# Hybrid SSD and attention block on one core: the weight sums' place, the tiles of the third product and the last block of S2

## The chip, the core and the metric

The kernel runs on one core of a Trainium2 chip. Its engines work side by side, each through its own list of instructions in a fixed order: TensorE (PE, matmuls and transposes, results go to PSUM), VectorE (DVE), ScalarE (ACT), GpSimd (POOL) and SyncE (SP, which here issues the DMA transfers). The metric is the device time of one execution in microseconds (us), the median over several. The profile is of one further execution; its span runs from the first to the last instruction.

## What is computed

One layer: a norm, an input projection, a state-space scan (SSD) over half of the channels, differential attention over the other half, gates, and an output projection of the two halves together, with a residual and a final norm. What the change touches is the attention and the output projection:

```python
def block(args):
    s = jnp.einsum('bhmqd,bhmkd->bhmqk', qblk, kh)        # two maps m per head
    s = jnp.where(dist >= 0, s + bias, -jnp.inf)
    p = jax.nn.softmax(s, axis=-1)
    w = p[:, :, 0] - lam * p[:, :, 1]
    return jnp.einsum('bhqk,bhke->bhqe', w, vh)
...
y_attn = attn.reshape(bsz, seq, D_ATTN) * jax.nn.silu(z_attn)
mixed = jnp.concatenate([y_ssd, y_attn], axis=-1)         # 1024 x 2048
h = h + jnp.einsum('bse,ed->bsd', mixed, w_out)           # w_out: 2048 x 1024
return rms_norm(h, final_norm_gain)
```

Sequence and model width are 1024, there are 8 heads, everything is float32.

## The kernel before

**Precision.** A float32 product is made of three matmuls of a reduced type: each operand is split into a high part (ACT copies it into that type) and a low part (DVE subtracts the high part), and hi x hi, hi x lo and lo x hi are summed in PSUM. So every operand passes over ACT and DVE before PE can use it. Names ending in `hi`/`lo` or `h`/`l` are these parts.

**Stages.** After the norm come the scan's two groups, then eight attention heads in four pairs, each head in two halves of 512 query rows, and then the output projection. `attend` handles a half head: four row blocks of 128 queries. For each of them PE makes the scores of both maps (L557) into two PSUM tiles S, DVE evicts them with the mask and takes the maximum (L563), ACT takes the exponential (L581), DVE combines the two maps (L594), PE transposes the result through the one PSUM bank `tp` (L602), ACT copies it out as `wT` (L605), and PE multiplies it with v (L609). At the end of a half head DVE copies the result out as `oc` (L614), and ACT sums its squares (L617). `gate` later multiplies with the gate z (L641), transposes (L647), and ACT writes `tTa` (L649), which goes to DRAM as a block of `tt_d` (L651). `tt_d` holds the transposed left operand of the output projection: 16 blocks of 128 channels, in two halves of the sequence; the last block of attention, 15, comes from the last head. Between the steps of softmax PE works on projections of the next heads, which fill its time.

**The output projection** is one step of Strassen's method in the Winograd form, with seven products of 512 x 1024 by 1024 x 512. Its left operands are A11, A12, A22 and the sums S1 to S4 of quarters of the left matrix, its right operands B11, B21, B22 and the sums T1 to T4 of quarters of `w_out`. They run in the order a11·b11, s3·t3, a12·b21, s2·t2, s1·t1, s4·b22, a22·t4 (`product`, matmuls at L757 to L759). A product has four row blocks `i` of 128, each of 8 x 3 matmuls of 512 columns, into the two PSUM banks `mm`. `find_t(k)` makes the sums T for one block of 128 rows: four loads into K tiles, four subtractions or additions on DVE (L673 to L679), each written to `t_d`. S3 is found from two loaded pieces when it is needed (L724) and written to `s3_d`; S2 is found from A22 and S3 (L735), S1 and S4 from S2 (L740, L745). `prep_b` and `prep_a` load and split operands (hi on ACT L689 and L710, lo on DVE L690 and L711). The first two products fill PE's time during the last head. Results are added to the rows `xr` of the residual on DVE (L821, L858, L860); `end_row` sums the squares and multiplies with the gain `fg` (L834), `finish` multiplies with the row's factor (ACT L841, DVE L843) and writes the output.

**What sets the order.** A scheduler in the recording layer puts the instructions of each engine in a list, by its own estimate of times, by the program's order as priority, and by when a tile's buffer comes free; on the chip each engine goes through its list strictly. Tiles come from pools of a fixed number of buffers: K (4 of 512 columns x 128), A (4), B (3), G (13), H (5), raw (2), u (4). All DMA transfers stand in SP's list, and one that has to wait holds up those behind it.

Of the kernel before, what the change touches and what calls it, by code (L numbers as in the profile page):

```python
# [38 lines left out]
def kernel(  # L39
# [595 lines left out]
    def gate(h, half, normed, z):  # L635
# [15 lines left out]
        dma(td[k], tT)  # L651
# [16 lines left out]
    def find_t(k):  # L668

        b11, b12, b21, b22 = (tK([P, HALF], name=f"b{i}{j}{k}") for i in range(1, 3) for j in range(1, 3))  # L670
        for raw, i, j in ((b22, 1, 1), (b12, 0, 1), (b11, 0, 0), (b21, 1, 0)):
# [1 line left out]
        V.tensor_tensor(b12, b22, b12, ALU.subtract)  # L673
# [6 lines left out]
        dma(t_d[1][k], b22)  # L680

    def prep_b(name, src, makers):

        hi, lo = (big_tile("u", 4, [P, NB, HALF], F32R, f"{name}_{n}") for n in ("hi", "lo"))
        for k in range(0, NB, 2):
            raw = makers[k // 2]([P, 2, HALF], name=f"r{name}{k}")
            dma(raw, src[k : k + 2].rearrange("a p c -> p a c"))
            cut = slice(k, k + 2)
            A.activation(hi[:, cut, :], raw, AF.Copy)  # L689
            V.tensor_tensor(lo[:, cut, :], raw, hi[:, cut, :].bitcast(F32), ALU.subtract)  # L690
        return hi, lo

    def load_a(raw, th, kh, q, k0, n):

        k = k0
        while k < k0 + n:
# [3 lines left out]
            dma(raw[:, k - k0 : e - k0, :], src.rearrange("k p s -> p k s"))  # L700
            k = e

    def prep_a(name, q, step, piece):
# [3 lines left out]
        for k0 in range(0, NB, step):  # L707
            raw = piece(q, k0, step)
            cut = slice(k0, k0 + step)
            A.activation(hi[:, cut, :], raw, AF.Copy)  # L710
# [62 lines left out]
    for p in range(HEADS // 2):  # L773
# [49 lines left out]
    def end_row(t, n, c0=0, c1=HALF):  # L823
# [10 lines left out]
        V.tensor_tensor(xt, xt, fg[:, n * HALF + c0 : n * HALF + c1], ALU.mult)  # L834

    def finish(t):
        r = sm.tile([P, 1], F32, tag="rs1", name=f"r_f{t}")
        G.tensor_tensor(r, ss[t][:, 0:1], half_pow[:, :1], ALU.pow)
# [90 lines left out]
```

## Time and profile before

| | us |
|---|---|
| median of three runs | 1047.63 |
| the three runs | 1046.67, 1047.63, 1049.41 |
| the profiled execution | 1046.4 |
| its span | 1044.3 |
| TensorE busy in it (last matmul ends at 1038.0) | 1006.9 |
| VectorE busy | 660.3 |
| ScalarE busy | 532.0 |
| mean granted TensorE clock (1 is full) | 0.993 |

The page of the profile shows the busy share of each engine in 40 slices of the span (26 us each), in tenths, 9 standing for 90% or more; under them the granted clock of TensorE, and the DMA engines:

```profile
PE   6999999999999989999999999999999999888997
DVE  6556578755566567476373772646816867579973
ACT  8253467834456434456353563535634755553352
PEclk9999999999999999999999999999999999999999
DMA  7111124211224787322103221023202447796432
```

The scan runs up to about 350 us, the heads up to 919, the last five products behind them. The heads are best read by who waited for whom, the ends by a timeline.

### The profile page before, as it was taken

To read this page: it belongs to the slowest core of one execution; us is meant where nothing else is said; L and a number is where in the kernel's file an instruction comes from. 1 tells how busy PE (TensorE), PEld (TensorE's weight loads), DVE (VectorE), ACT (ScalarE), POOL (GpSimd) and SP (SyncE) were. 2 spreads that over 40 slices of the span, in tenths; PEclk is the share of its full clock that TensorE was granted. 3 is DMA by queue.
4 is the path that set the end of the run, shared out by engine and by line. 5 is a ranking of instruction groups with operands and counts; after the bars stand their busy time and mean duration, and the time that the engine had idled before them with its cause. 6 is when DMAs were issued, how large, how long until landed. Compare 5 with 4: busy or idle time off the path is not lost.

```text
span 1044.3 us, 16231 instructions
## 1 busy us (share of the span) xinstructions
PE 1006.9 (96%) x6214; PEld 891.7 (85%) x6214; DVE 660.3 (63%) x1357; ACT 532.0 (51%) x1147; POOL 93.3 (9%) x133
## 2 busy tenths in 40 slices
PE   6999999999999989999999999999999999888997
PEld 5988888879997988889998889988899898766886
DVE  6556578755566567476373772646816867579973
ACT  8253467834456434456353563535634755553352
POOL 6000023200222100000000000000000000000011
PEclk9999999999999999999999999999999999999999
DMA  7111124211224787322103221023202447796432
GB/s 292 41 63 41 61 72 131 81 61 61 99 83 134 248 285 242 82 74 68 52 12 81 61 81 49 14 62 81 82 11 71 142 159 226 249 323 212 155 127 101
DMA packets 64948, 119.34 MB, mean 114 GB/s; under 512 B 5403, under 2 KB 30440, under 8 KB 64872
## 3 DMA queue, kind: packets, MB, share of 16 engines
q1 hardware_dynamic: 64872, 118.31, 34.9%
q8 instruction: 49, 0.80, 0.3%
q14 instruction: 27, 0.22, 0.1%
HBM read 86.77 MB, written 23.13 MB: 105 GB/s over the span
## 4 chain that ended last, share of the span: by engine, by line
PE 48%; DMA 8%; DVE 8%; issue 3%; ACT 2%; SPq 0%; POOL 0%; POOLq 0%; DVEq 0%; ACTq 0%
PE o L609 5%; PE mm L210 4%; PE mm L208 4%; PE mm L209 4%; PE mm L217 4%; PE mm L218 4%; PE mm L219 4%; PE S L557 4%; DMA ra<-tt_d 3%; PE mm L757 3%; PE mm L758 3%; PE mm L759 3%; DMA b<-in_w_out_dram 3%; PE tp L602 2%; DMA t_d<-b 1%
## 5 line engine op out<-in xcount | busy, mean ns | idle before, releaser
L581 ACT ACTIVATE s<-s,small 128x256 f32<-128x256 f32 (+7 forms) x128 | 98.7, 772 | 96.0 <-DVE small L573 95.5
L563 DVE CUSTOM_DVE_ANT_0 s<-S,dist 128x256 f32<-128x256 f32 (+7 forms) x128 | 94.2, 753 | 33.8 <-PE S L557 31.2
L208 PE MATMUL mm<-uh,hi_qk 128*128 128x512 f32 x256 | 101.5, 397 | 0.0
L210 PE MATMUL mm<-uh,lo_qk 128*128 128x512 f32 x256 | 101.0, 394 | 0.0
L209 PE MATMUL mm<-ul,hi_qk 128*128 128x512 f32 x256 | 100.7, 393 | 0.0
L557 PE MATMUL S<-k,q 128*128 128x512 f32 (+2 forms) x384 | 90.6, 358 | 4.7 <-DVE small L563 4.7
L605 ACT ACTIVATE wT<-tp 128x512 f32<-128x512 f32 (+2 forms) x96 | 46.5, 484 | 85.0 <-PE tp L602 84.7
L609 PE MATMUL o<-v,wT 128*128 128x128 f32 x576 | 81.5, 279 | 4.8 <-ACT wT L605 3.3
L609 PEld LDWEIGHTS o<-v,wT 128*128 128x128 f32 x576 | 75.9, 195 | 8.8 <-ACT wT L605 3.7
L557 PEld LDWEIGHTS S<-k,q 128*128 128x128 f32 x384 | 63.9, 190 | 14.0 <-DVE small L563 6.2
L217 PE MATMUL mm<-hi_v,uh 128*128 128x256 f32 x256 | 73.7, 288 | 0.2 <-DVE k L519 0.2
L219 PE MATMUL mm<-hi_v,ul 128*128 128x256 f32 x256 | 73.3, 287 | 0.0
L217 PE MATMUL mm<-hi_za,uh 128*128 128x256 f32 x256 | 73.3, 286 | 0.0
L218 PE MATMUL mm<-lo_za,uh 128*128 128x256 f32 x256 | 73.3, 286 | 0.0
L219 PE MATMUL mm<-hi_za,ul 128*128 128x256 f32 x256 | 73.0, 285 | 0.0
L218 PE MATMUL mm<-lo_v,uh 128*128 128x256 f32 x256 | 73.0, 285 | 0.0
L210 PEld LDWEIGHTS mm<-uh,lo_qk 128*128 128x128 f32 x256 | 48.1, 188 | 9.8 <-issue 0.2
L614 DVE TENSOR_SCALAR oc<-o 128x512 f32<-128x512 f32 x16 | 10.9, 684 | 71.3 <-PE o L609 71.0
L209 PEld LDWEIGHTS mm<-ul,hi_qk 128*128 128x128 f32 x256 | 48.2, 188 | 9.0
L208 PEld LDWEIGHTS mm<-uh,hi_qk 128*128 128x128 f32 x256 | 48.2, 188 | 8.9 <-issue 0.2
L217 PE MATMUL mm<-hi_z,uh 128*128 128x256 f32 x192 | 55.2, 287 | 0.0
L219 PE MATMUL mm<-hi_z,ul 128*128 128x256 f32 x192 | 55.0, 287 | 0.0
(270 smaller groups left out, 2704.6 us busy)
## 6 DMA issues: line engine op xcount, KB each, us to landing
m<-acs_d SPq DMA_DIRECT2D x16, 512.0 KB, 4.1
raw_qk<-in_w_blocks_dram SPq DMA_DIRECT2D x16, 512.0 KB, 4.8
q<-q SPq DMA_DIRECT2D x32, 256.0 KB, 3.1
b<-in_w_out_dram SPq DMA_DIRECT2D x32, 256.0 KB, 4.0
t_d<-b SPq DMA_DIRECT2D x32, 256.0 KB, 2.8
rt<-t_d SPq DMA_DIRECT2D x16, 512.0 KB, 4.7
ra<-tt_d SPq DMA_DIRECT2D x24, 256.0 KB, 3.9
rb<-in_w_out_dram SPq DMA_DIRECT2D x12, 512.0 KB, 4.7
```

The lines of the kernel that those rows point to most:

```text
L208: T.matmul(ps, hi[:, d, cut], uh[half][:, d, :], start=(d == 0), stop=False)
L209: T.matmul(ps, hi[:, d, cut], ul[half][:, d, :], start=False, stop=False)
L210: T.matmul(ps, lo[:, d, cut], uh[half][:, d, :], start=False, stop=(d == ND - 1))
L217: T.matmul(ps, uh[half][:, d, cut], hi[:, d, :], start=(d == 0), stop=False)
L218: T.matmul(ps, uh[half][:, d, cut], lo[:, d, :], start=False, stop=False)
L219: T.matmul(ps, ul[half][:, d, cut], hi[:, d, :], start=False, stop=(d == ND - 1))
L557: T.matmul(os[m], qs[half][m][:, part, qcut], ks[kh][:, m, :width], start=(part == 0), stop=(part == 1))
L563: V.tensor_tensor_reduce(out=s[:, :n], in0=ps[:, :n], in1=dist[:, S - n : S], op0=ALU.add, op1=ALU.max, scale=1.0, scalar=-3.0e38, accum_o ...
L581: A.activation(s[:, :n], s[:, :n], AF.Exp, bias=nb[:, m : m + 1], scale=slope, accum_out=sums[:, m, ii : ii + 1],)
L605: A.activation(wT[:, b0 : b0 + nb_, :], pt[:, : nb_ * P].rearrange("p (b c) -> p b c", c=P), AF.Copy)
L609: T.matmul(po[:, qcut], wT[:, kb, :], vs[kb // 4][:, kb % 4, vcut], start=(kb == 0), stop=(kb == i))
L757: T.matmul(ps[:, c0:c1], th[:, k, cut], bh[:, k, c0:c1], start=(k == 0), stop=False)
```

## The change

It has these parts:

- **Weight sums.** `find_t` becomes `sums_t`, a generator in two steps: the loads, then the four sums. `sums_s` does the same for S3, two blocks at a time, from whole blocks of `tt_d`. `next_sums` is called behind each half head: it makes the sums of the block that was loaded at the last call, and starts the next block's loads. `pin` keeps the first sum and the loads in the program's order among themselves. So there are twelve blocks (eight of T, four of S3) over twelve half heads, from the second on.
- **S3 product.** `piece_s3` now loads S3 from `s3_d`; the results `p7` of this product lie in G in place of K.
- **a12 product**, the third to run. Its operands are prepared ahead of the last gate; the pieces of a12 are of two blocks, in K (where the scan has its state tiles), in place of four blocks in B.
- **S2.** `find_s2` finds blocks 0 to 6 of S2 ahead of the last gate, in A tiles. Block 7 needs the last head's block 15: `gate` computes it from the transposes' PSUM bank itself, minus `s3_last`, behind `s2_found`. `prep_a` takes cut lists, so that block 7 is split by itself (`BY4_LAST`).
- **Transfers.** `gate` issues the write of `tTa` from ACT in place of SP. `dma_next` chains the loads of the products in the program's order. The weights' raw tiles for the last four products are raw (2 blocks) and K (1 block), in place of raw and G.
- **End.** The row block that `product` splits in two takes one PSUM bank for each piece. For all rows but the last, the gain `fg` goes into `finish` as one instruction with the row's factor on DVE; in the last row the two output halves change engines. `fg` is loaded later.

The number of matmuls stays. The diff, cut:

```diff
@@ gate
-        dma(td[k], tT)
+        A.dma_start(td[k], tT)
+        if h == HEADS - 1 and half == 1:
+            with tc.issue_after(s2_found):
+                for q in range(2):
+                    cut = slice(q * 256, (q + 1) * 256)
+                    V.scalar_tensor_tensor(
+                        s2[q, 4][:, 3, :], pt[:, cut], g8, s3_last[0][:, cut], op0=ALU.mult, op1=ALU.subtract
+                    )
...
+    def pin(ins):
+        return tc.keep_in_program_order(ins)
+
-    def find_t(k):
+    def sums_t(k):
         b11, b12, b21, b22 = (tK([P, HALF], name=f"b{i}{j}{k}") for i in range(1, 3) for j in range(1, 3))
         for raw, i, j in ((b22, 1, 1), (b12, 0, 1), (b11, 0, 0), (b21, 1, 0)):
-            dma(raw, w_quarter(i, j)[k])
-        V.tensor_tensor(b12, b22, b12, ALU.subtract)
+            pin(dma(raw, w_quarter(i, j)[k]))
+        yield
+        pin(V.tensor_tensor(b12, b22, b12, ALU.subtract))
         dma(t_d[3][k], b12)
...
+    def sums_s(k):
+        a11, a21 = ([tK([P, HALF], name=f"a{i}1{k + n}") for n in range(2)] for i in range(1, 3))
+        for half, raws in enumerate((a11, a21)):
+            for n, raw in enumerate(raws):
+                td, j = tt_of(k + n, 4 * half)
+                pin(dma(raw, td[j]))
+        yield
+        pin(V.tensor_tensor(a11[0], a11[0], a21[0], ALU.subtract))
+        dma(s3_d[k], a11[0])
+        V.tensor_tensor(a11[1], a11[1], a21[1], ALU.subtract)
+        dma(s3_d[k + 1], a11[1])
+        yield
+
+    sums = [sums_t(k) for k in range(NB)] + [sums_s(k) for k in range(0, NB, 2)]
+    begun = []
+    def next_sums():
+        if begun:
+            next(begun.pop())
+        if sums:
+            begun.append(sums.pop(0))
+            next(begun[0])
...
     def piece_s3(q, k0, n):
-        raw, sub = piece_of(0, 0, tK)(q, k0, n), piece_of(1, 0, tK)(q, k0, n)
-        V.tensor_tensor(raw, raw, sub, ALU.subtract)
-        dma(s3_d[q][k0 // 2], raw)
+        raw = tK([P, n, 256], name=f"s3{q}{k0}")
+        load_s3(raw, q, k0, n)
         return raw
...
+    def find_s2():
+        s3_last.append(tH([P, HALF], name="s3_last"))
+        dma(s3_last[0], s3_d[NB - 1])
+        for q in range(2):
+            for k0, n in ((0, 4), (4, 3)):
+                raw = s2[q, k0] = tA([P, 4, 256], name=f"s2{q}{k0}")
+                load_a(raw[:, :n, :], 1, 1, q, k0, n)
+                sub = (raw_tile if (q, k0) == (1, 4) else tB)([P, n, 256], name=f"s3b{q}{k0}")
+                load_s3(sub, q, k0, n)
+                found = V.tensor_tensor(raw[:, :n, :], raw[:, :n, :], sub, ALU.subtract)
+        return found.ins
+
     def piece_s2(q, k0, n):
-        raw = s2[q, k0] = piece_of(1, 1, tA)(q, k0, n)
-        sub = tB([P, n, 256], name=f"s3{q}{k0}")
-        for k in range(0, n, 2):
-            dma(sub[:, k : k + 2, :], s3_d[q][(k0 + k) // 2])
-        V.tensor_tensor(raw, raw, sub, ALU.subtract)
-        return raw
+        return s2[q, k0 // 4 * 4][:, k0 % 4 : k0 % 4 + n, :]
...
@@ product
-            ps = ps_mm()
             for c0, c1 in pieces if i == 3 else ((0, HALF),):
+                ps = ps_mm()
...
@@ heads
-        even = [run(h, half, qkc, vs, (1,)) for half in range(2)]
+        even = []
+        for half in range(2):
+            even.append(run(h, half, qkc, vs, (1,)))
+            next_sums()
...
             waiting.append((h + 1, half, run(h + 1, half, qkc, vs, at), zs[half]))
-        for k in range(3 * p, min(NB, 3 * p + 3)):
-            find_t(k)
-    while waiting:
+            next_sums()
+    while len(waiting) > 1:
         gate(*waiting.pop(0))
...
-    p7 = [tK([P, HALF], name=f"p7{i}") for i in range(4)]
+    p7 = [tG([P, 2, HALF], name=f"p7{q}") for q in range(2)]
...
+    b2 = prep_b("b21", w_quarter(1, 0), [(raw_tile, 2)] * 4)
+    a2 = [prep_a("a12", q, BY2, piece_of(0, 1, tK)) for q in range(2)]
+    b_raws = [(raw_tile, 2), (tK, 1), (tK, 1)] * 2
...
+    queued.append(None)
+    s2_found = find_s2()
+    gate(*waiting.pop(0))
...
@@ end_row
-        V.tensor_tensor(xt, xt, fg[:, n * HALF + c0 : n * HALF + c1], ALU.mult)
+        if t == NT - 1:
+            V.tensor_tensor(xt, xt, fg[:, n * HALF + c0 : n * HALF + c1], ALU.mult)
@@ finish
-            if n == 0:
-                A.activation(xts[t][:, n, :], xts[t][:, n, :], AF.Copy, scale=r)
+            if t < NT - 1:
+                V.scalar_tensor_tensor(xt, xt, r, fg[:, n * HALF : (n + 1) * HALF], op0=ALU.mult, op1=ALU.mult)
+            elif n == 0:
+                V.tensor_scalar(xt, xt, r, None, ALU.mult)
             else:
-                V.tensor_scalar(xts[t][:, n, :], xts[t][:, n, :], r, None, ALU.mult)
+                A.activation(xt, xt, AF.Copy, scale=r)
```

How the lists of the engines change at three places; numbers in names are of buffers, sizes are partitions x columns. First DVE at the start of the first head, before. `b` are the tiles of the weight sums, `s` and `small` those of softmax, `S` the scores in PSUM:

```order
L563 ISA s_3465,small_3458<-S,dist 128x128
L563 ISA small_3458 128x1
L673 TENSOR_TENSOR b_4476<-b_4478,b_4476 128x512
L573 TENSOR_SCALAR small_3458<-small_3458 128x1
L675 TENSOR_TENSOR b_4475<-b_4476,b_4475 128x512
L677 TENSOR_TENSOR b_4477<-b_4477,b_4475 128x512
L679 TENSOR_TENSOR b_4478<-b_4478,b_4475 128x512
L673 TENSOR_TENSOR b_4492<-b_4494,b_4492 128x512
L675 TENSOR_TENSOR b_4491<-b_4492,b_4491 128x512
L677 TENSOR_TENSOR b_4493<-b_4493,b_4491 128x512
```

and DVE at the same place in the changed kernel:

```order
L563 ISA s_3458,small_3451<-S,dist 128x128
L563 ISA small_3451 128x1
L563 ISA s_3462,small_3451<-S,dist 128x128
L563 ISA small_3451 128x1
L573 TENSOR_SCALAR small_3451<-small_3451 128x1 x2
L200 TENSOR_TENSOR lo_qk_3996<-raw_qk_3997,hi_qk_3995 128x8x128
L200 TENSOR_TENSOR lo_qk_3996<-raw_qk_3999,hi_qk_3995 128x8x128
L563 ISA s_3481,small_3474<-S,dist 128x256
```

Before, three blocks of sums stood between the evictions of the first row block's two maps; now the evictions follow each other, and no sum stands in the first head.

Second PE at the end of the last head, before: `tp` from `s` are the transposes of softmax, `o` the products with v, `tp` from `t` those of a gate, `a12` the first operand of the product that follows the heads:

```order
L759 MATMUL mm<-t_hi,s3l_8905 128x512
L602 MATMUL tp<-ident,s_8607 128x128 x2
L609 MATMUL o<-v_7461,wT_8618 128x128 x4
L609 MATMUL o<-v_7562,wT_8618 128x128 x2
L602 MATMUL tp<-ident,s_8646 128x128 x7
L609 MATMUL o<-v_7461,wT_8657 128x128 x4
L609 MATMUL o<-v_7562,wT_8657 128x128 x3
L647 MATMUL tp<-ident,t_8676 128x128 x4
L602 MATMUL tp<-ident,s_8700 128x128 x8
L609 MATMUL o<-v_7461,wT_8711 128x128 x4
L609 MATMUL o<-v_7562,wT_8711 128x128 x4
L757 MATMUL mm<-b_hi,a12h_9081 128x512
```

and PE in the changed kernel:

```order
L609 MATMUL o<-v_7498,wT_8659 128x128 x4
L827 MATMUL mm<-b_lo,a12h_9058 128x512
L828 MATMUL mm<-b_hi,a12l_9059 128x512
L826 MATMUL mm<-b_hi,a12h_9058 128x512
L827 MATMUL mm<-b_lo,a12h_9058 128x512
L828 MATMUL mm<-b_hi,a12l_9059 128x512
L826 MATMUL mm<-b_hi,a12h_9058 128x512
L827 MATMUL mm<-b_lo,a12h_9058 128x512
L828 MATMUL mm<-b_hi,a12l_9059 128x512
L609 MATMUL o<-v_7599,wT_8659 128x128 x2
L602 MATMUL tp<-ident,s_8687 128x128 x7
L609 MATMUL o<-v_7498,wT_8698 128x128 x4
```

Eight matmuls of the a12 product (blocks 0 to 5 of the first two row blocks) now stand between the two parts of a row block's product with v; 28 more stand ahead of these, and the list behind is as before.

Third DVE in the stretch of the S2 product, before; `p<-p,mm` reads the PSUM bank of the product's first two row blocks, `t_lo` are conversions for the next product, `ra<-ra,ra` finds S1:

```order
L740 TENSOR_TENSOR ra_9430<-ra_9430,ra_9257 128x1024
L690 TENSOR_TENSOR t_lo<-rt_9407,t_hi 128x1024
L690 TENSOR_TENSOR t_lo<-rt_9411,t_hi 128x1024
L740 TENSOR_TENSOR ra_9437<-ra_9437,ra_9268 128x1024
L690 TENSOR_TENSOR t_lo<-rt_9415,t_hi 128x1024
L690 TENSOR_TENSOR t_lo<-rt_9419,t_hi 128x1024
L711 TENSOR_TENSOR s2l_9267<-ra_9276,s2h_9266 128x1024
L829 TENSOR_SCALAR ssf<-ssf 128x1
L834 TENSOR_TENSOR xr_9052<-xr_9052,fg 128x512
L858 TENSOR_TENSOR p_8764<-p_8764,mm 128x512 x2
```

and DVE in the changed kernel:

```order
L768 TENSOR_TENSOR s2l_9305<-s_9129,s2h_9304 128x256
L746 TENSOR_TENSOR t_lo<-rt_9292,t_hi 128x512
L746 TENSOR_TENSOR t_lo<-rt_9436,t_hi 128x1024
L902 TENSOR_SCALAR ssf<-ssf 128x1
L746 TENSOR_TENSOR t_lo<-rt_9440,t_hi 128x512
L746 TENSOR_TENSOR t_lo<-rt_9444,t_hi 128x512
L746 TENSOR_TENSOR t_lo<-rt_9448,t_hi 128x1024
L746 TENSOR_TENSOR t_lo<-rt_9452,t_hi 128x512
L746 TENSOR_TENSOR t_lo<-rt_9456,t_hi 128x512
L809 TENSOR_TENSOR ra_9462<-ra_9462,s_9114 128x1024
L931 TENSOR_TENSOR p_8792<-p_8792,mm 128x512 x2
```

The multiplication with `fg` (L834) is gone from this stretch, and two of the sums for S1 now stand behind `p<-p,mm` (L931); the six conversions `t_lo` of the next product still stand ahead of it.

More of the change, by code (lines that the diff above doesn't have):

```diff
@@ L650, in gate @@
         td, k = tt_of(8 + h, 4 * half)
-        dma(td[k], tT)
+        A.dma_start(td[k], tT)
[6 more added lines that the diff above has]
+                    )
     NB = 8
     t_d = {n: dram.tile([NB, P, HALF], F32, name=f"t_d{n}") for n in (1, 2, 3, 4)}
-    s3_d = [[dram.tile([P, 2, 256], F32, name=f"s3_d{q}{k}") for k in range(0, NB, 2)] for q in range(2)]
+    s3_d = dram.tile([NB, P, HALF], F32, name="s3_d")
     def w_quarter(kh, nh):
@@ L680, in find_t, with raw_tile, dma_next, b_tiles @@
         dma(t_d[1][k], b22)
-    def prep_b(name, src, makers):
[L684 to L688, printed above, removed]
+        yield
[10 more added lines that the diff above has]
+        dma(s3_d[k + 1], a11[1])
+        yield
+    sums = [sums_t(k) for k in range(NB)] + [sums_s(k) for k in range(0, NB, 2)]
[6 more added lines that the diff above has]
+            next(begun[0])
+    def raw_tile(shape, dt=F32, name=None):
+        return big_tile("raw", 2, shape, dt, name)
+    queued = []
+    def dma_next(dst, src):
+        if queued and queued[0] is not None:
+            with tc.issue_after(queued[0]):
+                queued[0] = dma(dst, src).ins
+        else:
+            ins = dma(dst, src).ins
+            if queued:
+                queued[0] = ins
+    def b_tiles(name):
+        return [big_tile("u", 4, [P, NB, HALF], F32R, f"{name}_{n}") for n in ("hi", "lo")]
+    def prep_b(name, src, makers):
+        hi, lo = b_tiles(name)
+        k = 0
+        for make, n in makers:
+            raw = make([P, n, HALF], name=f"r{name}{k}")
+            dma_next(raw, src[k : k + n].rearrange("a p c -> p a c"))
+            cut = slice(k, k + n)
             A.activation(hi[:, cut, :], raw, AF.Copy)
             V.tensor_tensor(lo[:, cut, :], raw, hi[:, cut, :].bitcast(F32), ALU.subtract)
+            k += n
         return hi, lo
@@ L712, in prep_a @@
         return hi, lo
+    BY2, BY4, BY4_LAST = (0, 2, 4, 6, 8), (0, 4, 8), (0, 4, 7, 8)
     def piece_of(th, kh, make):
@@ L853 @@
         end_row(i, 0)
-    b6 = prep_b("t2", t_d[2], makers)
-    a6 = [prep_a("s2", q, 4, piece_s2) for q in range(2)]
+    b6 = prep_b("t2", t_d[2], b_raws)
+    a6 = [prep_a("s2", q, BY4_LAST, piece_s2) for q in range(2)]
     for i, _, _, ps in product(a6, b6):
@@ L859 @@
         add(i, 1, u)
-        V.tensor_tensor(u, u, p7[i], ALU.add)
+        V.tensor_tensor(u, u, p7[i // 2][:, i % 2, :], ALU.add)
         add(4 + i, 1, u)
         add(4 + i, 0, u)
-    b5 = prep_b("t1", t_d[1], makers)
-    a5 = [prep_a("s1", q, 4, piece_s1) for q in range(2)]
+    fg = tG([P, D], name="fg")
+    dma_next(fg, bass.AP(vectors.tensor, vectors.offset + 304, [[0, P], [1, D]]))
+    b5 = prep_b("t1", t_d[1], b_raws)
+    a5 = [prep_a("s1", q, BY4, piece_s1) for q in range(2)]
     for i, _, _, ps in product(a5, b5):
@@ L868 @@
         end_row(4 + i, 1)
-    b3 = prep_b("b22", w_quarter(1, 1), makers)
-    a3 = [prep_a("s4", q, 4, piece_s4) for q in range(2)]
+    b3 = prep_b("b22", w_quarter(1, 1), b_raws)
+    a3 = [prep_a("s4", q, BY4, piece_s4) for q in range(2)]
     for i, _, _, ps in product(a3, b3):
@@ L874 @@
         finish(i)
-    b4 = prep_b("t4", t_d[4], makers)
-    a4 = [prep_a("a22", q, 4, piece_of(1, 1, tB)) for q in range(2)]
+    b4 = prep_b("t4", t_d[4], b_raws)
+    a4 = [prep_a("a22", q, BY4, piece_of(1, 1, tB)) for q in range(2)]
     for i, c0, c1, ps in product(a4, b4, ((0, 256), (256, HALF))):
```

34 lines of the change are left out of this document (15 added, 19 removed).

## The prediction

> **What bounds the kernel now.** I read the head of the page first, then who waited for whom on PE, then the stretches in which PE stood.
>
> ```profile
> span 1044.3 us, 16231 instructions
> PE 1006.9 (96%) x6214; PEld 891.7 (85%) x6214; DVE 660.3 (63%) x1357; ACT 532.0 (51%) x1147; POOL 93.3 (9%) x133
> ```
>
> PE is busy 1006.9 of 1044.3 us, and the change adds and removes no matmul. So what it can win is the 37.4 us in which PE has nothing, plus time that PE is busy at a lower clock. The waits of PE say where these lie (engine and line, waited for: us in total, times, longest):
>
> ```profile
> PE S L187 <- DVE x L183: 8.9, 4, 7.3
> PE S L557 <- DVE small L563: 4.7, 3, 3.6
> PE mm L757 <- DVE p L858: 3.9, 1, 3.9
> PE o L609 <- ACT wT L605: 3.3, 2, 1.8
> PE tp L602 <- ACT wT L605: 1.4, 2, 0.7
> PE mm L757 <- DVE xr L821: 1.4, 2, 0.8
> PE mm L757 <- ACT a12h L710: 1.2, 1, 1.2
> ```
>
> The first row is the start of the program, which the change leaves alone. The rest is four places: the first attention head (3.6, 1.8), the end of the last head (1.5 of the 3.3, then 1.4 and 1.2), the S2 product (3.9) and the end. The stretches (us; busy time and count of PE, PEld, DVE, ACT, POOL; granted clock; DMA share, GB/s) show the middle and the clock:
>
> ```profile
> 374.72:378.13 3.41, 2.92 (x12) 2.92 (x13) 3.41 (x11) 0.99 (x4) 0.00 (x0) 0.50 1.00 324
> 613.00:747.00 134.00, 133.65 (x904) 122.92 (x904) 75.92 (x217) 66.27 (x156) 4.81 (x8) 1.00 0.19 55
> 800.00:900.00 100.00, 99.46 (x568) 86.38 (x567) 71.53 (x174) 59.78 (x130) 3.90 (x6) 1.00 0.55 175
> 906.92:910.61 3.69, 1.50 (x11) 1.27 (x12) 2.14 (x2) 2.05 (x4) 0.00 (x0) 1.00 0.77 213
> 910.61:914.03 3.42, 3.42 (x18) 3.42 (x17) 0.00 (x0) 0.49 (x1) 0.00 (x0) 0.50 1.01 353
> 940.00:960.00 20.00, 16.13 (x70) 13.05 (x69) 19.88 (x24) 10.04 (x13) 0.00 (x0) 0.96 0.67 211
> 958.40:961.81 3.41, 2.94 (x7) 2.39 (x8) 3.41 (x5) 0.00 (x0) 0.00 (x0) 0.50 0.66 218
> 980.00:1000.00 20.00, 20.00 (x90) 16.55 (x89) 19.91 (x27) 10.49 (x16) 0.00 (x0) 1.00 0.42 141
> ```
>
> Between the heads PE is full (133.65 of 134.00) with DVE at 57% and ACT at 49%. Three times, just after PE stood, the clock is 0.50 for 3.41 us: each such dip costs 1.7 us more than the wait itself.
>
> **The first head (7.2 us fall away).** Weight sums stand between the softmax steps on DVE and wait there for their loads.
>
> ```profile
> L673 DVE TENSOR_TENSOR b<-b,b 128x512 f32<-128x512 f32 x7 | 4.8, 693 | 21.6 <-DMA b<-in_w_out_dram 18.3 <-issue 3.3
> 375.21 0.58 PE L557 MATMUL S<-k,q 128*128 128x256 f32 x1 [3.63 <-DVE small L563]
> 402.24 0.60 PE L609 MATMUL o<-v,wT 128*128 128x128 f32 x3 [1.84 <-ACT wT L605]
> ```
>
> DVE stood 21.6 us ahead of seven first sums, between 340 and 415. The eviction of S (L563) is queued behind them, and so PE waited 3.63 and 1.84 us, with the first dip after it. In the new order no sum stands in the first head at all. So 3.63 + 1.84 + 1.71 = 7.2 go, and what is late next there is PE's own work. Bounds: nothing won, if another wait of that size takes their place, to 7.2.
>
> **The sums in the later heads (cost 1.0 us).** Eight blocks of four subtractions (693 ns each, 2.8 us a block) and four of two (1.4) come into twelve half heads: 28 us of DVE, which takes its 57% to about 71%. The cover is PE's projections between the steps of softmax. A block's load has to be there when DVE reaches it:
>
> ```profile
> b<-in_w_out_dram SPq DMA_DIRECT2D x32, 256.0 KB, 4.0
> t_d<-b SPq DMA_DIRECT2D x32, 256.0 KB, 2.8
> tt_d<-tTa SPq DMA_DIRECT2D x16, 256.0 KB, 2.1
> ra<-tt_d SPq DMA_DIRECT2D x8, 128.0 KB, 3.6
> SPq L651 <- ACT tTa L649: 163.2, 13, 18.9
> ```
>
> A block's four buffers are those of the block before, so a load starts when the four results are written: 2.8 + 4.0 = about 7 us after the last block, where a half head lasts some 16 (134 us hold eight). So DVE should not stand for loads, and SP does not stand 163.2 us for tTa any more, as ACT issues those sixteen writes. They cost ACT an issue each of about 0.3 us, behind which an exp or a copy waits; ACT is half idle, so nothing of it reaches PE, but if that cover fails it is 16 x 0.3 = 5 us. The blocks themselves cost between nothing and 12 x 2.8 = 34 us, if each moved the softmax chain by its full length; the nearest row, 800 to 900 us with DVE at 71.5%, has PE idle 0.5 us, and so I take 1.0 for the 200 us of twelve half heads.
>
> **The end of the last head and the S2 product (wins 3.7 us).** Rows of PE:
>
> ```profile
> 908.42 0.71 PE L609 MATMUL o<-v,wT 128*128 128x128 f32 x4 [1.50 <-ACT wT L605]
> 910.66 3.20 PE L609 MATMUL o<-v,wT 128*128 128x128 f32 x14
> 917.11 2.01 PE L609 MATMUL o<-v,wT 128*128 128x128 f32 x16
> 920.32 0.50 PE L757 MATMUL mm<-b_hi,a12h 128*128 128x512 f32 x1 [1.20 <-ACT a12h L710]
> 958.87 0.76 PE L757 MATMUL mm<-t_hi,s2h 128*128 128x512 f32 x1 [3.87 <-DVE p L858]
> ```
>
> The last product of the head ends at 919.12. Ahead of it now stand 36 matmuls of the a12 product, eight of them in the place of the 1.50 us wait. At 90 matmuls in 20 us they take 8.1 us; the wait goes, and with it the dip (fourteen products took 3.20 at half clock, sixteen 2.01 behind it). So the head ends at 919.1 + 8.1 - 1.5 - 1.7 = 924.0. The two waits for the one transpose bank (1.4) stay: the order there is the same.
>
> The next matmul needs blocks 6 and 7 of a12, and block 7 comes out of that head's first half: its copy (0.7, 512 columns), its write (2.1) and its load (3.6) end 6.4 us after the transposes, which stand 4.7 ahead of the last product's end. On ACT its conversion comes behind two steps of the square sum, which wait for that end: the copy of o 0.7, two steps of 0.3 and their readouts 0.8, the conversion about 0.6. So PE starts 2.1 to 2.9 us after 924.0; I take 2.9, where it stood 1.20 before. What counts then is DVE (the last row is the square sum on ACT):
>
> ```profile
> 906.70 2.36 DVE L690 TENSOR_TENSOR t_lo<-rt,t_hi 128x1024 fp32r<-128x1024 f32 x2 [2.53 <-ACT t_hi L689]
> L834 DVE TENSOR_TENSOR xr<-xr,fg 128x512 f32<-128x512 f32 x4 | 2.7, 681 | 0.0
> L821 DVE TENSOR_TENSOR xr<-xr,mm 128x512 f32<-128x512 f32 x4 | 2.6, 682 | 0.1
> 924.22 0.17 DVE L630 TENSOR_SCALAR sso<-sso 128x4 f32<-128x4 f32 x1
> 926.31 0.16 DVE L632 TENSOR_TENSOR r_o<-r_o,keep 128x4 f32<-128x4 f32 x1
> 922.34 0.29 ACT L617 ACTIVATE junk<-oc 128x128 bf16<-128x128 f32 x1
> ```
>
> From the copy of o to the first p<-p,mm (the read that frees the bank for the third row block of S2) the new order has on DVE 8 instructions of 1024 columns at 1.14 (two in 2.36, the start of the second hidden), 20 of 512 at 0.60, 4 of 768 at 0.87 (between the two), 4 of 256 at 0.33, the gate's four (1.1) and nine small ones (0.9): 9.1 + 12.0 + 3.5 + 1.3 + 1.1 + 0.9 = 27.9. It also waits: 1.3 for the late a12h, and some 2 around r_o, which came 1.9 us after its input. That is 31.2, so that PE gets its bank at 924.0 + 31.2 = 955.2. PE itself would be there after 2.9 + 108 matmuls (24.2) + the last transposes 0.6 = 27.7, at 951.7. So it stands 3.5 us, much as it does now (3.87), and the dip behind it stays. The gain is 958.9 - 955.2 = 3.7. Taking the four L834 and two subtractions of S2 out of this stretch, as the change does, shortens DVE's list, but all six conversions of the next product's weights now stand ahead of p<-p,mm. Bounds: 0, if transfers (353 GB/s here) hold DVE up by as much again, to 8.9, if neither wait nor dip is left.
>
> [...]
>
> **The end (wins 1.1 us).**
>
> ```profile
> 1034.44 0.41 DVE L821 TENSOR_TENSOR xr<-xr,mm 128x256 f32<-128x256 f32 x1
> 1034.91 0.39 PE L757 MATMUL mm<-t_hi,a22h 128*128 128x256 f32 x1 [0.78 <-DVE xr L821]
> 1040.08 0.72 ACT L841 ACTIVATE xr<-xr,r_f 128x512 f32<-128x512 f32 x1 [0.97 <-POOL r_f L838]
> 1040.08 0.49 DVE L843 TENSOR_SCALAR xr<-xr,r_f 128x512 f32<-128x512 f32 x1 [0.44 <-POOL r_f L838]
> ```
>
> The last row block's second half had to wait 0.78 for the add that reads the first half's bank (0.41, at 1034.44); now it has a bank of its own, free long before. And the first output half comes from DVE (0.49) in place of ACT (0.72), so both writes start 0.2 to 0.3 earlier. From 0.2 to 1.1. The gain of fg folded into the last multiply is off PE's path: DVE is 19.91 of 20 busy at 980 to 1000 while PE never stands.
>
> **Sum.** 7.2 - 1.0 + 3.7 + 1.1 = 11.0. The profiled execution took 1046.4 us (span 1044.3 and 2.1 around it), so it would be 1035.4; the median of the three runs, 1047.6, lies 1.2 above that execution, which gives **1036.6**.
>
> **Rivals.** (A) *The change does all it says*: S2 no longer stands, the dip is gone too. That is 3.5 + 1.7 better, 1031.4. For it: blocks 0 to 6 of S2 are found ahead, block 7 comes straight from the bank. Against it: the list of DVE above, which no longer holds a wait but is as long. (B) *It wins only part*: the S2 stretch gives nothing back (1036.6 + 3.7), or the first head finds a new wait of 3.6 with its dip (+ 5.3): 1040 to 1042, and with both 1045.6, which is no change. For it speaks that DVE is full in the whole stretch of S2 (19.88 of 20.00 at 940), so any added wait there goes to PE. (C) *Slower*: the pinned sums hold up every softmax they stand in. Place: the S eviction L563 behind four subtractions. Price: the first head's own row, 3.63 with its dip 5.3 a block if loads are late, or up to 2.8 a block if they aren't. From 11.0 / 12 = 0.9 us a block the kernel is slower; at 2 us a block it takes 1036.6 + 23 = 1060. Against it: 7 us of transfers in 16, and PE's full rows while DVE was 71.5% busy.
>
> **Chances.** Forecast 0.53; (A) 0.17; (B) 0.22, of it 0.12 under 1044.5 and 0.10 around no change; (C) 0.08. About 0.3%, 3 us, is what a measurement here can tell from no change. Faster by more: 0.53 + 0.17 + 0.12 = 0.82; same 0.10; slower 0.08. The range goes from the better part of (A), 1029.5, to 1044: beyond it lie (C), the part of (B) around no change and a small part of (A), 0.2 in all. The bounds of the terms lead there too: S2 at its best 5.2 lower and sums at no cost 1.0 lower is 1030.4, the first head at nothing 1043.8.
>
> **What would show it.** In the new profile: no DVE wait for b<-in_w_out_dram over 1 us, and no PE wait or dip between 340 and 415 (else the first step is wrong). Sums in the later heads without PE waits over 1 us (else C). The a12 product in the place of the 1.50 wait, then a wait of 2 to 3 us ahead of the first a12 matmul behind the head. A PE wait of about 3.5 us in S2 for DVE's p<-p,mm; if it is under 1 us, (A) holds. No wait between the last two pieces. Wrong would be above all a PE wait that I name nowhere: for the a12 or S2 transfers, or for q in a head, whose copies now stand behind the sums' transfers on SP.

## The result and the profile after

The changed kernel takes 1035.02 us (median of four runs, 1033.82 to 1036.12), the kernel before in the same session 1047.15 (1046.34 to 1049.41). The ratio is 0.988, with a 95% interval of 0.986 to 0.9901, so 12 us or 1.2% less, faster beyond what the measurement leaves uncertain. The forecast was 1036.6 in a range of 1029.5 to 1044. The profiled execution took 1034.4 us against 1035.4 forecast.

The head of the page of the changed kernel, in the form shown before:

```profile
span 1032.7 us, 16261 instructions
PE 1001.8 (97%) x6214; PEld 888.9 (86%) x6214; DVE 661.4 (64%) x1366; ACT 528.6 (51%) x1154; POOL 92.0 (9%) x133
```

The span is 11.6 us shorter. PE's time without work falls from 37.4 to 30.9, and PE is busy 5.1 us less with the same 6214 matmuls; one dip of the clock less (two in place of three; a dip lasted 3.41 us at a clock of 0.50, as from 604.95 to 608.36) is 1.7 of these, and the other 3.4 stand at no one place. Who waited for whom on PE (engine and line, waited for: us in total, times, longest):

```profile
PE S L187 <- DVE x L183: 8.9, 4, 7.4
PE tp L602 <- ACT wT L605: 3.5, 3, 2.1
PE mm L826 <- DVE p L931: 2.5, 1, 2.5
PE mm L826 <- ACT a12h L767: 2.2, 1, 2.2
PE mm L826 <- DVE xr L894: 1.4, 1, 1.4
PE o L609 <- ACT wT L605: 1.0, 2, 0.5
...
PE S L557 <- DVE small L563: 0.6, 2, 0.4
```

The 4.7 us for `small`, 4.2 of them in the first head, are down to 0.6, none of it there, and the 3.9 for `p<-p,mm` to 2.5. New are a single wait of 2.1 for the transpose bank `tp`, and one of 1.4 for `xr` in the s1 product; the wait for `a12h` grew from 1.2 to 2.2. The first head is seen best in the stretch from 340 to 415 us (the kernel before first; busy time and count of PE, PEld, DVE, ACT, POOL, the granted clock, DMA share, GB/s):

```profile
340.00:415.00 75.00, 68.40 (x516) 65.02 (x515) 48.86 (x117) 28.77 (x72) 2.94 (x6) 0.98 0.79 261
```

and the changed kernel:

```profile
340.00:415.00 75.00, 75.00 (x571) 71.86 (x570) 39.92 (x102) 36.38 (x86) 4.10 (x7) 1.00 0.22 65
```

PE does 55 matmuls more in the same 75 us, at full clock. The first sums of each block of T (L684) no longer wait for a load anywhere, where DVE had stood 21.6 us ahead of seven:

```profile
L684 DVE TENSOR_TENSOR b<-b,b 128x512 f32<-128x512 f32 x8 | 5.5, 685 | 0.0
```

The sums for S3 do wait: four times, 8.2 us in all and 4.3 the longest (at 690), DVE stands ahead of one (L704) for its load. No wait of PE stands behind these four.

The remaining waits of PE, from its timeline (start, us, engine, line, operation; in brackets the wait before it and for whom):

```profile
604.13 0.33 PE L602 MATMUL tp<-ident,s 128*128 128x128 f32 x1 [2.14 <-ACT wT L605]
914.48 2.01 PE L609 MATMUL o<-v,wT 128*128 128x128 f32 x16
918.72 0.60 PE L826 MATMUL mm<-b_hi,a12h 128*128 128x512 f32 x1 [2.23 <-ACT a12h L767]
948.08 0.50 PE L826 MATMUL mm<-t_hi,s2h 128*128 128x512 f32 x1 [2.46 <-DVE p L931]
971.54 0.47 PE L826 MATMUL mm<-t_hi,s1h 128*128 128x512 f32 x1 [1.37 <-DVE xr L894]
```

How the gain builds up is read by setting the same matmul of both timelines side by side:

| place | before | after | gained so far | forecast |
|---|---|---|---|---|
| scan, first product behind the wait for `cbm` | 219.00 | 218.46 | 0.5 | 0 |
| second head pair, products of one row block (L609) | 582.42 | 572.79 | 9.6 | 7.2 |
| end of the last head's last product | 919.12 | 916.49, with 36 matmuls (8.1) more ahead of it | 10.7 | 9.4 |
| third row block of S2 starts | 958.87 | 948.08 | 10.8 | 9.9 |
| 54 matmuls on, at the start of the s1 product | 972.61 | 960.49 | 12.1 | 9.9 |
| behind the new wait in the s1 product | 982.81 | 972.31 | 10.5 | 9.9 |
| end of the last matmul | 1038.05 | 1026.54 | 11.5 | 11.0 |

### The profile page after: what moved, and what is told of

The parts are those of the page before. It is cut to its first block, busy times and chain, and to the rows that moved or that the text cites. A ratio compares the mean times of both kernels' runs of the same rounds, so it can differ in the third digit from the quotient of the medians.

```text
span 1032.7 us, 16261 instructions
## 1 busy us (share of the span) xinstructions
PE 1001.8 (97%) x6214; PEld 888.9 (86%) x6214; DVE 661.4 (64%) x1366; ACT 528.6 (51%) x1154; POOL 92.0 (9%) x133
## 4 chain that ended last, share of the span: by engine, by line
PE 91%; ACT 3%; DVE 3%; issue 1%; DMA 1%; POOL 0%; POOLq 0%; SPq 0%; ACTq 0%; DVEq 0%
PE mm L208 10%; PE mm L209 10%; PE mm L210 10%; PE mm L217 8%; PE mm L218 8%; PE mm L219 8%; PE S L557 6%; PE o L609 6%; PE mm L826 4%; PE mm L827 4%; PE mm L828 4%; PE tp L602 3%; PE S L439 3%; PE S L448 1%; PE S L452 1%
## 5 line engine op out<-in xcount | busy, mean ns | idle before, releaser
L609 PE MATMUL o<-v,wT 128*128 128x128 f32 x576 | 80.2, 276 | 1.0 <-ACT wT L605 1.0
L609 PEld LDWEIGHTS o<-v,wT 128*128 128x128 f32 x576 | 75.1, 192 | 5.1 <-ACT wT L605 1.9
L218 PE MATMUL mm<-lo_z,uh 128*128 128x256 f32 x192 | 54.9, 286 | 0.0
```

The lines of the kernel that those rows point to most:

```text
L218: T.matmul(ps, uh[half][:, d, cut], lo[:, d, :], start=False, stop=False)
L609: T.matmul(po[:, qcut], wT[:, kb, :], vs[kb // 4][:, kb % 4, vcut], start=(kb == 0), stop=(kb == i))
```

## The experiments

The theory was the forecast's own: order on DVE's list, not DVE's amount of work, makes the waits of the heads, and in the S2 stretch DVE is full, so that its list sets PE. Twelve runs were made in three sessions, each beside the kernel before (medians there 1048.27, 1047.20 and 1047.30); one of them is the changed kernel itself.

**The sums alone** (`e1_sums_only`): the kernel before with this part of the change and nothing else.

```diff
-        for k in range(3 * p, min(NB, 3 * p + 3)):
-            find_t(k)
+            next_sums()
```

> The kernel before with one part of the change alone: the weight sums and the sums for S3, one block behind each half head, and S3 loaded where it is needed; nothing else of the change. If the first step is right, the two waits of the first head (3.63 and 1.84 us) and the dip behind the first (1.71) are gone, no PE wait over 1 us stands between 340 and 420, and the sums cost 1 to 3 us in the later heads: 1041 to 1043 where the kernel before takes 1047. The rival: the sums need SP free of the tTa writes, which stay on SP here; then a block's loads stand behind them, DVE waits for b by more than 1 us in several half heads, PE waits with it, and the time is 1046 or more.

Measured: 1042.27 us, ratio 0.9947 (0.9932 to 0.9963). No wait of PE over 1 us is left between 340 and 420, though tTa is still written from SP. So the first step needs the sums' new place only. The wait at 602 comes with this part as well, with 1.96 us; the 2.2 in the first row is another one, at 900, with a dip behind it, and the changed kernel hasn't got it:

```profile
PE tp L602 <- ACT wT L605: 5.6, 4, 2.2
PE mm L788 <- DVE p L891: 4.9, 1, 4.9
```

The S2 product still waits 4.9 here, with 6.83 us of half clock: that part of the gain is made by the rest of the change. Which of the rest makes it (the tiles of a12, S2 found ahead, the raw tiles, `fg`) was not run apart.

**The sums' arithmetic left out** (`e7_no_t_sums`).

```diff
-        pin(V.tensor_tensor(b12, b22, b12, ALU.subtract))
         dma(t_d[3][k], b12)
-        V.tensor_tensor(b11, b12, b11, ALU.add)
```

> The changed kernel with the 32 subtractions and additions of the T sums left out (the loaded quarters are written as they are; the eight instructions for S3 stay). If DVE's time for the sums costs the 3.8 us of waits between 460 and 740 (0.38, 0.44, 2.14, 0.26, 0.55) and half a dip, these go: 1030 to 1031. If the 2.14 at 602 is a matter of the order that the scheduler gave ACT and DVE there (no sum stands within 17 us ahead of it), it stays or goes whatever DVE's time, and the small ones alone go: 1033 to 1035.

Measured: 1049.36 us, ratio 1.0017 (0.9998 to 1.0035), 14 us *slower* than the changed kernel, with 20 us less work on DVE (641.6 in place of 661.4). Neither theory had this. The pinned instruction went with the arithmetic, so the loads and writes of all eight blocks ran off one behind the other, up to 397 us, and the scheduler put a subtraction for S3 (L700) into the first head:

```profile
407.75 0.69 DVE L700 TENSOR_TENSOR a<-a,a 128x512 f32<-128x512 f32 x1 [13.71 <-DMA a<-tt_d]
408.36 0.15 DVE L573 TENSOR_SCALAR small<-small 128x1 f32<-128x1 f32 x1
```

and on PE:

```profile
410.37 0.80 PE L609 MATMUL o<-v,wT 128*128 128x128 f32 x2 [10.44 <-ACT wT L605]
```

DVE stands 13.71 us ahead of one sum of 0.69, the softmax's `small` is behind it, and PE stands 10.44 us; its clock is at half until 413.3. This shows the first step's mechanism, and what rival (C) feared of a late load, without any load of DVE. What it was made for, the cost of the sums' own time, it can't tell.

**The writes of tTa on SP again** (`e2_tta_sp`).

```diff
-        A.dma_start(td[k], tT)
+        dma(td[k], tT)
```

> The changed kernel with the writes of tTa on SP again. The prediction held that neither side matters: ACT's sixteen issues of 0.3 us are covered, and SP's waits for tTa delay nothing that PE needs. Then 1034 to 1036 and the same waits. The rival: a sum's loads, or the last gate's block, stand behind a tTa write on SP, which gives DVE waits for b or a12h later than 918.7, and 1037 or more.

Measured: 1035.91 us, ratio 0.9902 (0.9887 to 0.9916). In the heads all is as in the changed kernel, but for the wait at 602: 1.96 here and in e1, which both write tTa from SP, and 2.14 in the changed kernel. So ACT's sixteen issues (0.33 us each in the changed kernel) cost PE 0.2 us at most there. But the a12 wait grew:

```profile
PE mm L826 <- ACT a12h L767: 4.1, 1, 4.1
...
PE mm L826 <- DVE xr L894: 2.5, 1, 2.5
...
PE mm L826 <- DVE p L931: 0.9, 1, 0.9
```

The rival was right that SP's list is the reason, but it was not block 7 that came late. DVE shows what did:

```profile
915.68 1.23 DVE L801 TENSOR_TENSOR s<-s,s3b 128x1024 f32<-128x1024 f32 x1 [16.83 <-DMA s3b<-s_d]
916.82 0.68 DVE L614 TENSOR_SCALAR oc<-o 128x512 f32<-128x512 f32 x1
```

The load of `s3b` for S2 stands in SP's list behind the write of tTa, which waits for ACT: it is issued at 911.74, where the changed kernel issues it at 908.26. DVE waits for it with a subtraction of S2, and the copy of o stands behind, 1.5 us after PE had done with o (915.27); ACT's square sums and the conversion of `a12h` follow on that copy. It is e7's mechanism once more. Of the 1.9 us more, 1.6 came back in S2 (0.9 in place of 2.5), and the s1 product waits 1.1 more: 7.5 in place of 6.1 for the three. So in the traces the issue from ACT is worth 1.4 us (2.2 against the changed kernel's second profile), at the last write but one; the intervals of the measured times overlap.

**The t1 conversions later** (`e5_t1_late`, then `e8_t1_s1_late`).

```diff
-        V.tensor_tensor(u, u, ps, ALU.add)
+        reads.append(V.tensor_tensor(u, u, ps, ALU.add).ins)
...
-    b5 = prep_b("t1", t_d[1], b_raws)
+    with tc.issue_after(reads[0]): b5 = prep_b("t1", t_d[1], b_raws)
```

> The changed kernel; DVE's conversions of the next product's weights (six t_lo of t1) stand behind the first p<-p,mm of the S2 product instead of ahead of it. If the wait there is only a matter of their order on DVE, the 2.46 us go, nothing takes their place, and the time is 1032.5. The rival: DVE is full from 925 to 990, so that the conversions are missed later: the wait for xr ahead of the s1 product (1.37 at 970) grows to 3 or 4 us, and the time stays at 1034 to 1035.

Measured: 1037.23 us, ratio 0.9904 (0.9874 to 0.9933), nothing won. The S2 wait stayed at 2.08, and the waits in the s1 product came to 1.44 and 2.33. With the conversions gone from the list, an addition for S1 stood first, and its load was late:

```profile
943.48 1.23 DVE L809 TENSOR_TENSOR ra<-ra,s 128x1024 f32<-128x1024 f32 x1 [3.95 <-DMA ra<-tt_d]
944.63 0.68 DVE L931 TENSOR_TENSOR p<-p,mm 128x512 f32<-128x512 f32 x1
```

So e5 could not tell the theories apart. In e8 the additions for S1 stand behind `p<-p,mm` too:

```diff
+    with tc.issue_after(reads[0]): a5 = [prep_a("s1", q, BY4, piece_s1) for q in range(2)]
```

> As e5_t1_late, with DVE's work for S1 also behind the first p<-p,mm, since in e5 an addition for S1 stood first in the list and waited 3.95 us for its load. Now only the read of the bank comes next. If order alone makes the S2 wait, it is under 0.5 (from 2.46) and the wait at the s1 product stays at 1.4: PE waits behind 900 of 5.8, 1032.5. If DVE's load makes it, the S2 wait goes too, but the waits in the s1 product grow to 3.5 or 4: 8 us in all, 1034 to 1036.

Measured: 1035.54 us, where the changed kernel took 1034.49 in the same session (`e0_changed`). The S2 wait is down to 0.33, and this took its place (the second of two, the other is 0.59):

```profile
PE mm L828 <- DVE s1l L768: 3.7, 2, 3.1
```

The waits from S2 on are 0.33 + 0.59 + 3.14 + 0.37 = 4.4 us, against 2.46 + 1.37 = 3.8 and 2.29 + 0.79 = 3.1 in the changed kernel's two profiles. So the S2 wait is a matter of order, and in this order its price came back in the s1 product. That no order is free of both is not shown, for DVE was not full here:

```profile
945.53 0.69 DVE L931 TENSOR_TENSOR p<-p,mm 128x512 f32<-128x512 f32 x1 [3.07 <-PE mm L828]
```

The edit holds all six conversions back until that read, and DVE stands 3.07 us, though ACT had made the first of their high parts by 941.7. That is about what the s1 product then waits (3.14). And between `s1h` (ready on ACT at 970.8) and the `s1l` that PE waits for (974.26), DVE works on other additions and on conversions for the product behind. An order with a conversion or two in the 3.07 us was not run.

**The t1 conversions on POOL** (`e9_t1_pool`, with the additions for S1 late as in e8).

```diff
-    b5 = prep_b("t1", t_d[1], b_raws)
+    b5 = prep_b("t1", t_d[1], b_raws, G)
```

> The changed kernel with the six conversions of t1 on POOL in place of DVE (4.5 us of DVE's list), and DVE's work for S1 behind the first p<-p,mm. If DVE's load from 925 to 990 sets both waits, the S2 wait (2.46) and the s1 wait (1.37) are both under 0.5 and PE's waits behind 900 fall from 8.2 to about 4.5: 1031. The rival, that the transfers of t1 and S1 are late in themselves, leaves 2 us or more of waits there; a second, that POOL (2.6 us for 1024 columns by its rows of 1.3 for 512) is late with t1, shows as a wait of the s1 product for POOL.

Measured: 1035.74 us, ratio 0.9889 (0.9869 to 0.991). The S2 wait is 0.33, but one of 2.37 for a later `p<-p,mm` stands 11 us on. POOL's six conversions (min, median, max in ns):

```profile
L746 POOL TENSOR_TENSOR t_lo<-rt,t_hi x6: 1267/2006/3384, 938.8 to 949.0; 128x512 fp32r<-128x512 f32 x4, 128x1024 fp32r<-128x1024 f32 x2
```

and DVE beside them:

```profile
943.46 1.57 DVE L809 TENSOR_TENSOR ra<-ra,s 128x1024 f32<-128x1024 f32 x1
944.96 0.67 DVE L931 TENSOR_TENSOR p<-p,mm 128x512 f32<-128x512 f32 x1
945.55 2.30 DVE L894 TENSOR_TENSOR xr<-xr,p 128x512 f32<-128x512 f32 x1
947.77 2.30 DVE L809 TENSOR_TENSOR ra<-ra,s 128x1024 f32<-128x1024 f32 x1
...
951.71 1.21 DVE L809 TENSOR_TENSOR ra<-ra,s 128x1024 f32<-128x1024 f32 x1
```

An addition of 512 columns takes 2.30 (the next, at 950, 1.78) in place of 0.68, one of 1024 up to 2.30 in place of 1.21, until POOL is done at 951. So four instructions took 4.2 us more than alone (0.4, 1.6, 1.1, 1.1), of the 4.7 that the move had taken off DVE (two conversions at 1.14, four at 0.60). So POOL is no place for this work while DVE adds beside it.

**The early gate** (`e4_gate_early`, and once more as `e4_again`): the transposes of the gate of the last head's first half go ahead of the last two row blocks.

```diff
+                with tc.issue_after(gate_pe[0]) if (h, half) == (HEADS - 1, 1) and ii >= 2 else ExitStack():
...
+            gate_pe[0] = T.transpose(pt[:, cut], tt[:, cut], ident).ins
...
-            at = (2,) if last and half else (2, 3)
+            at = (1,) if last and half else (2, 3)
```

> The changed kernel; in the last head the gate of that head's first half is transposed ahead of the last two row blocks instead of ahead of the last one, so that block 7 of a12 is written and loaded earlier. Both theories expect the wait for a12h (2.23) and the dip behind it (1.7) to be gone. If it was DVE's list from the copy of o on that sets the end of the S2 product's first half (third step of the prediction), the S2 wait for p<-p,mm grows in return from 2.5 to 5 or 6 us and the time stays within 1 us of the changed kernel's 1035. If PE's own work sets it, the gain stays: 1031.

> The early gate once more, in more rounds, beside the others here. Its waits of PE sum up as in the changed kernel (25.2 against 25.0 us), but the wait for a12h is 0.9 us in place of 2.2. If a dip needs about 1.9 us idle in one window of 3.41, the early gate has one place less for a dip, 0.56 x 1.7 = 1 us on the mean: 1033 to 1034.5. If its first median of 1032.1 comes from a shorter path instead, it stays 2.5 us ahead of the changed kernel.

Measured: 1032.12 us, ratio 0.9859 (0.9834 to 0.9884), and again 1032.44, 0.9861 (0.9841 to 0.9881). The changed kernel's own second measurement (`e0_changed`) gave 1034.49, 0.9876 (0.9854 to 0.9898).

> The changed kernel itself once more, on the chip of the next three, so that small differences can be told. Expected 1034 to 1036, and PE waits behind 900 us of 8.2 in all (0.69, 0.78, 0.69, 2.23, 2.46, 1.37) as in its first profile. The dips of the clock should fall on other waits than 602 and 916: if they stand on a fixed grid of 3.41 us whose phase differs from execution to execution, a wait of about 2 us has a dip behind it in some executions and none in others.

The waits of PE behind 900 in this second profile come to 7.5 us in place of 8.2. Its dips stand behind the a12 wait and the S2 wait (917.45 and 948.17), and none at 602, where the first profile had one.

In the repeated run the a12 wait is 0.97 us, less than half, as expected, the S2 wait 2.18 and the one in s1 1.81. The S2 wait did not grow to 5 or 6, but neither was the edit clean: the scheduler put twelve more a12 matmuls (48 in place of 36) ahead of the head's last product, so that DVE copies o later, with part of the a12 product's work done before. In the first run of it:

```profile
920.28 0.68 DVE L614 TENSOR_SCALAR oc<-o 128x512 f32<-128x512 f32 x1
943.95 0.68 DVE L931 TENSOR_TENSOR p<-p,mm 128x512 f32<-128x512 f32 x1
```

That is 23.7 us from the one to the other, where the changed kernel has 30.8. So this run does not test the third step as it was meant to. In the medians the early gate is 2 us ahead, though the intervals overlap. The profiled executions don't show a shorter path: without their dips (two, two, none, one, at 1.7 each) the last matmul ends at 1023.1 and 1022.8 in the changed kernel and at 1023.5 and 1023.4 here. Whether it is faster, and by what, stays open.

**Two combinations.** `e6_both` is the early gate with e5, `e10_pool_gate` the early gate with e9 and eight more additions on POOL.

> Both edits together: the early gate and the late conversions of t1. If each only removes a wait of its own, 1035.0 - 3.9 - 2.5 = 1028.6. If the early gate alone gains nothing because DVE's list comes last, but that list is shorter here by the six conversions (4.5 us), the S2 wait is under 2 us and the time 1029 to 1031. If DVE as a whole is the bound from 925 to 990, the time is 1033 to 1035 and the lost time stands ahead of the s1 product.

> e9_t1_pool and the early gate of e4 together, with eight of the additions to xr behind the S2 product on POOL too (5.4 us less on DVE). If DVE's load is what took back the gain of the early gate, the wait for a12h is under 1 us and the waits in S2 and s1 are under 1.5 together: PE waits behind 900 of 4 us, and 1028 to 1030, faster than e4_gate_early by 2 or more. If not, 1031 to 1033 as e4.

Measured: 1033.96 us, ratio 0.9876 (0.9846 to 0.9906), and 1040.62, ratio 0.9939 (0.9917 to 0.9961). In e6 the S2 wait is 0.55, and 3.14 stand in the s1 product for `s1l`, as in e8. In e10, with eight additions (15 us) more on POOL, the waits for `p<-p,mm` and `xr` are 5.4 and 4.5 us: as in e9, longer instructions on DVE while POOL works, over more than twice the time (27.0 us of POOL in place of 12.4). From 939 to 976 DVE's additions and subtractions take 11 us longer in sum than alone, where the move had taken 9.5 off it.

**One bank for both pieces** (`e3_one_bank`).

```diff
+            ps = ps_mm()
             for c0, c1 in pieces if i == 3 else ((0, HALF),):
-                ps = ps_mm()
```

> The changed kernel with one PSUM bank for both pieces of a product's last row block, as before. The fourth step gives 0.78 us to the second bank: a wait of PE of 0.78 for xr between the last two pieces comes back, and the time is 0.8 more, 1035.5. The rival: the gain came from the swap of the output halves, or from nothing, and this is the changed kernel's time with no wait there.

Measured: 1035.61 us, ratio 0.9899 (0.9884 to 0.9914). The wait is back ahead of the last piece, with 1.39 us; with two banks there is none. It is more than the 0.78 of before because two of the new multiplications with factor and `fg` (1.41) stand on DVE ahead of the addition that frees the bank.

## The prediction's steps against the runs

**The first head: right in kind, 7.2 against about 9.** All three parts went (no wait, clock 1.00 from 340 to 415). Between the scan and the second head pair 9.1 us were gained; three smaller waits of before that the forecast did not count (0.22, 0.52, 0.42) went too, against two new ones (0.38, 0.44). Some 1.6 us of it are in no wait that the trace names, and stay open. e1 shows that the place of the sums alone does it, e7 that a single sum ahead of its load brings it back.

**The sums in the later heads: the mechanism was wrong, and the size too small.** The 1.0 us stood for DVE's load. Small waits of PE are there (0.38, 0.44, 0.26, 0.55), but four of 0.4 to 0.5 were there before too, and what part the sums have in them is not shown. What cost more is the 2.14 at 602, with a dip 3.8 us in place of 1.0. No sum stands within 17 us ahead of it; the lists of DVE and ACT around it are in another order:

```profile
600.39 1.22 DVE L200 TENSOR_TENSOR lo_za<-raw_za,hi_za 128x1024 fp32r<-128x1024 f32 x1
601.53 0.14 DVE L573 TENSOR_SCALAR small<-small 128x1 f32<-128x1 f32 x1
```

and on ACT:

```profile
601.71 1.04 ACT L581 ACTIVATE s<-s,small 128x896 f32<-128x896 f32 x1 [0.43 <-DVE small L573]
602.66 0.19 ACT L581 ACTIVATION_READ_ACCUMULATOR s<-s,small 128x1 f32 x1
602.87 0.59 ACT L507 ACTIVATE q<-mm 64x512 fp32r<-64x512 f32 x1
603.48 0.60 ACT L605 ACTIVATE wT<-tp 128x512 f32<-128x512 f32 x1
```

The copy `wT`, for which PE waits with its one transpose bank full, stands behind an exponential and a copy of q. Before, at the same place, it stood ahead of that exponential:

```profile
611.76 0.60 ACT L605 ACTIVATE wT<-tp 128x512 f32<-128x512 f32 x1
612.32 0.59 ACT L518 ACTIVATE k<-mm 64x512 fp32r<-64x512 f32 x1
612.82 1.03 ACT L581 ACTIVATE s<-s,small 128x896 f32<-128x896 f32 x1
```

In the changed kernel's profile a dip followed. No run puts the old order back, so that the order alone makes this wait is read from the lists. Rival (C), a stall in each block, did not come: the loads of T were there, and where S3's were late, PE had nothing behind them.

**The end of the head and S2: the ledger held, the clock did not.** The head's end was forecast at 924.0 - 7.2 + 1.0 = 917.8 and came at 916.49. The two waits for `tp` stayed (0.78, 0.69, and 0.69 ahead of them). The a12 wait was 2.23 (bounds 2.1 to 2.9, I took 2.9): ACT's steps behind the copy of o set it, not the load. DVE's list from the copy of o to `p<-p,mm` was forecast at 31.2:

```profile
916.53 0.69 DVE L614 TENSOR_SCALAR oc<-o 128x512 f32<-128x512 f32 x1 [3.14 <-PE o L609]
947.34 1.28 DVE L931 TENSOR_TENSOR p<-p,mm 128x512 f32<-128x512 f32 x2
```

It took 30.8 to the start of the first of the two, and 31.5 to its end, which the forecast's count of instructions takes in. PE stood 2.46 there and not 3.5, since a dip behind the a12 wait had slowed PE itself by 1.7 (918.98 to 922.39). I had said that the dip behind S2 stays and that the one at the head's end goes; in this profile it was the other way round, and in that of e0 both came. Two things came out otherwise than the term of 3.7: the step from the second head pair to S2 gave only 1.2 (10.8 - 9.6; forecast -1.0 + 3.7 = 2.7), of which the wait at 602 and its dip are the main part, and behind S2 1.3 came on top with before's dip there gone. A wait that I named nowhere followed, the 1.37 at 970, which took 1.6 back. It fits what spoke against rival (A): from 945 to 975 DVE is busy 30.00 of 30.00 us. But e8 shows no more than that one other order brings the price back.

**The end: right but for the swap.** 1.1 forecast, 1.0 measured (10.5 to 11.5). The second bank carries it (e3). The swapped output halves, of which I took up to 0.3, give less than 0.1: from the last matmul to the span's end it takes 6.26 us before and 6.19 after.

**The sum** of 11.0 came near the 11.6 of the span (12.0 between the profiled times) in part by luck, because errors of 1 to 3 us cancelled: more from the first head, less from the later heads, a dip gone and a new wait.

## What to carry to other kernels

An instruction that waits for a transfer costs what is queued behind it, whatever it costs itself: a sum of 0.7 us held PE up by 10.4 us (e7), and a late load of S2 made the wait for a12 longer (e2), while four late loads of S3 cost PE nothing, since nothing that it needed stood behind. So look first for the places where the engine that is waited for stands idle itself, and move the waiting instruction, with its loads, to where they have time; and read the new list for the next instruction that waits (e5). Where an engine is full over a whole stretch, a wait that is removed by order can come back a little later (e8); see whether the new order leaves the engine idle before you conclude that only less work helps.

## What was not expected of the hardware

**Dips of the clock stood on a grid.** In each of three profiles they began a whole number of 3.413 us apart: before at 374.72, 910.61 and 958.40 (157 and 14 steps), in the changed kernel at 604.95 and 918.98 (92), in its second measurement at 917.45 and 948.17 (9). Cutting the first two of these profiles on that grid, from 230 us to the last matmul, PE stood 1.91 us or more in five windows (those from 371.31, 907.20 and 954.99 before, from 601.53 and 915.56 after), and a dip of one window followed each time; in twelve it stood 0.52 to 1.80 us, and no dip followed. The same S2 wait in two executions of the changed kernel, first the window with most of the wait, then the next one (the column after POOL is the clock):

```profile
946.28:949.69 3.41, 1.61 (x7) 1.34 (x8) 3.41 (x6) 1.06 (x1) 0.00 (x0) 1.00 0.53 184
949.69:953.11 3.42, 3.42 (x17) 2.81 (x16) 3.42 (x5) 1.06 (x1) 0.00 (x0) 1.00 0.00 0
```

and in the second measurement:

```profile
944.76:948.17 3.41, 1.35 (x6) 1.14 (x7) 3.06 (x5) 1.06 (x1) 0.00 (x0) 1.00 0.72 239
948.17:951.59 3.42, 3.42 (x10) 2.64 (x9) 3.28 (x4) 1.06 (x1) 0.00 (x0) 0.50 0.01 4
```

In the first the wait of 2.46 is split by the grid into 0.67 and 1.80, and costs no dip; in the second 2.06 of 2.29 fall into one window. So the same wait of 2.3 to 2.5 us had a dip behind it in one execution and none in the other. By my estimate from these windows it was luck, too, that the kernel before had its dip at the head's end in the profile from which the forecast took it off (1.91 us idle in its window, the least of the five).

**POOL and DVE were slower side by side** (e9, POOL busy from 938.8 to 951.2): an addition on DVE took 2.30 us in place of 0.68, a conversion of 512 columns on POOL 1.74 and 2.27 in place of 1.27 and 1.30, while `p<-p,mm`, with one operand in PSUM, kept its 0.67 (at 944.96). What makes both slower was not shown.
